# Stick-breaking attention on one core: value products ordered behind the scores of the unit five places later

## The chip, the cores and the metric

The kernel runs on one core of a Trainium2 chip. The metric is device time in microseconds (us) for one execution. A core has TensorE (PE, matrix products; PEld is its weight load), VectorE (DVE), ScalarE (ACT), GpSimd (POOL) and SyncE (SP, which here issues nearly all DMAs), each with its own in-order queue of instructions.

## The reference, cut to what matters

One layer on a sequence of 2048 positions and width 1024: RMS norm, one projection, four heads of differential attention and eight heads of stick-breaking attention, output projection with residual, and a SwiGLU feed-forward part. The part around the change is stick-breaking attention, per head and query `t`:

```python
z = jnp.einsum('bqhd,bkhd->bhqk', qb, k) * scale
mask = k_pos < q_pos                                   # strictly causal
log_1mb = jnp.where(mask, jax.nn.log_sigmoid(-z), 0.0)
rem = lax.cumsum(log_1mb, axis=3, reverse=True) - log_1mb
a = jnp.where(mask, jnp.exp(jax.nn.log_sigmoid(z) + rem), 0.0)
y = jnp.einsum('bhqk,bkhd->bqhd', a, v)
```

Each weight is thus sigmoid(z) times the product of sigmoid(-z) over the keys between it and the query.

## The kernel before, in words

The work is one stream without barriers, in two scopes. The first holds projections, attention and output projection, the second the feed-forward part, as products of 2x2 blocks. Products are made in float16 from operands that are split in a high and a low half, with three products for one.

Attention runs over eight groups `g` (`for g in range(NG)`, line 792). Groups 0 to 3 are the differential heads (`diff_attn`, line 460), groups 4 to 7 are pairs of stick-breaking heads (`sb_attn`, line 536). While a group is attended to, `advance` (line 708) emits the projection tiles of the next groups (`proj_tile`, line 313: 24 products of 384 columns at line 320 for each tile of 128 positions). In the last group the output projection (line 761) is emitted beside the attention.

A stick-breaking group is walked in 48 **units** (lines 577 to 587): for each of 16 query blocks `i` of 128 rows, for each 1024-column part `b` of the keys from the diagonal back, for each of the two heads `m`. A unit goes through these steps:

- `stage_a` (line 540), in chunks of up to 512 columns from the right: `score_chunk` (line 446) makes the scores in a PSUM tile `sc` (two products at line 448, and at the diagonal a third, line 450, that masks); ScalarE makes sigmoid(-z) into the SBUF tile `om` (line 554) and sigmoid(z) in place (line 555); VectorE scans the product from right to left (line 557) and multiplies (line 558). There are four `sc` tiles, and nine tiles `z4` for the `om` and `be` of all units.
- `split_t` (line 398): ScalarE casts the weights to float16 (line 89), GpSimd makes the low half (line 98), both in one of three buffers `s`; SP issues a DMA transpose into one of six buffers `aT` (line 403).
- `stage_b` (line 565), the unit's **values**: `pv` (line 453) multiplies `aT` by the values `v` into the PSUM tile `yp`, three products of 64 columns for each 128 keys (line 458, up to 24 for a unit); after the last unit of a row of query blocks `finish` (line 407) norms, transposes and stores to `ms`, which the output projection loads again.

The loop holds five units back in `pend` (`PD` = 5, line 39): it calls `stage_b` of a unit only after `stage_a` of the unit five places later. That is the order in which the program is written, not the order on the engines. The kernel is built with a scheduler that plays through an estimate of all durations and gives each engine, whenever it is free in that play, the ready instruction of highest priority. Priorities follow the written order, moved by the table `PRI` (line 32): `at` = 200 lifts all of `stage_a` ahead, and `pm` = -200 puts the projection products back; values (`pv` = 0) keep their place. So values can come out on TensorE ahead of scores of later units or behind them, and projections fill in.

What the scheduler makes is fixed at build time. On the chip every engine runs its list in order: an instruction whose input is late holds up all behind it on that engine.

Of the kernel before, what the change touches and what calls it, by code (L numbers as in the profile page):

```python
# [21 lines left out]
S, D, P = 2048, 1024, 128  # L22
# [37 lines left out]
def block(tc, a, out):  # L60
    nc = tc.nc
    PE, ACT, DVE, POOL, SP = nc.tensor, nc.scalar, nc.vector, nc.gpsimd, nc.sync
    top = ExitStack()
    with top:
# [186 lines left out]
        with ExitStack() as ph1:  # L251
# [189 lines left out]
            def fq(g, i):  # L441
                k = 2 if g == NG - 1 else 4
                return (i % k, k)

            @pri("sc")
            def score_chunk(G, sc, i, q, m, w, cut=False):
                for o in range(2):
                    PE.matmul(sc[:, : 128 * w].rearrange("p (t n) -> p t n", n=P), lhsT=G["q"][i // 4][:, 2 - 2 * o + m, i % 4, :], rhs=G["k"][q][:, m, 0:w, :], start=o == 0, stop=o == 1)  # L448
                if cut:
                    PE.matmul(sc[:, 128 * w - P : 128 * w], lhsT=idb[:], rhs=tri[:], start=False, stop=True, skip_group_check=True)  # L450

            @pri("pv")
            def pv(G, yp, y0, aT, b, n, o, wd, start, stop):
# [81 lines left out]

            def sb_attn(g, G):
                last = {}

                @pri("at")
                def stage_a(i, m, b):  # L540
                    L = (i + 1) * 128
                    n = min(1024, L - 1024 * b)
                    be, om = z4(), z4()
                    if b == i // 8:
                        DVE.memset(om[:, n : n + 1], 8192.0)
                    else:
                        DVE.tensor_copy(om[:, n : n + 1], last[m][:, 0:1])
                    last[m] = om
                    for c in range((n - 1) // 512, -1, -1):
                        lo, hi = 512 * c, min(512 * c + 512, n)  # L550
                        w = hi - lo
                        sc = ps.tile([P, 512], F32, tag="sc", bufs=4, name=nm("sc"))
                        score_chunk(G, sc, i, 2 * b + c, m, w // P, b == i // 8 and hi == n)
                        ACT.activation(om[:, lo:hi], sc[:, :w], AF.Sigmoid, scale=G["nkz"][:])  # L554
                        ACT.activation(sc[:, :w], sc[:, :w], AF.Sigmoid, scale=G["kz"][:])  # L555
                        ov = om[:, lo:hi][:, ::-1]
                        DVE.tensor_tensor_scan(ov, ov, sc[:, :w], om[:, hi : hi + 1], op0=ALU.mult, op1=ALU.bypass)  # L557
                        DVE.tensor_tensor(be[:, lo:hi], sc[:, :w], om[:, lo + 1 : hi + 1], ALU.mult)  # L558
# [669 lines left out]
```

## Time and profile before

| what | value |
|---|---|
| time, median of 3 runs (lowest, highest) | 2731.22 us (2727.44, 2734.09) |
| time of the profiled execution | 2740.3 us |
| its span, first to last instruction | 2738.5 us |
| mean granted TensorE clock | 0.967 |
| differential groups | until about 603 us |
| stick-breaking beside projections | about 603 to 1190 us |
| last group beside output projection | about 1190 to 1400 us |
| rest of output projection | to about 1458 us |
| feed-forward part | to the end |

An engine's busy time is the union of its instructions' times. A row of waits reads: engine, tile and line that waited, `<-` what ended the wait, then us in total, times, and the longest. A row of a timeline reads: start in us, duration in us, engine, line, operation, tiles written `<-` tiles read, shapes, count, and in brackets the engine's idle time before it and what ended it. Tile names come without numbers, so `z` stands for `om` and `be` of every unit, and `s` for the buffers of the cast. The end of an idle time is told by semaphores: where TensorE waits for a free `sc` tile, the row names the VectorE instruction that was last counted, which may be line 545, 547 or 558.

### The profile page before, as it was taken

To read this page: it belongs to the slowest core of one execution; us is meant where nothing else is said; L and a number is where in the kernel's file an instruction comes from. 1 tells how busy PE (TensorE), PEld (TensorE's weight loads), DVE (VectorE), ACT (ScalarE), POOL (GpSimd) and SP (SyncE) were. 2 spreads that over 40 slices of the span, in tenths; PEclk is the share of its full clock that TensorE was granted. 3 is DMA by queue.
4 is the path that set the end of the run, shared out by engine and by line. 5 is a ranking of instruction groups with operands and counts; after the bars stand their busy time and mean duration, and the time that the engine had idled before them with its cause. 6 is when DMAs were issued, how large, how long until landed. Compare 5 with 4: busy or idle time off the path is not lost.

```text
span 2738.5 us, 45414 instructions
## 1 busy us (share of the span) xinstructions
PE 2490.0 (91%) x17084; PEld 1409.8 (51%) x17084; DVE 1978.5 (72%) x3752; ACT 1353.3 (49%) x2539; POOL 1429.8 (52%) x1002
## 2 busy tenths in 40 slices
PE   7998989898978886889989898999999999999999
PEld 4655656565545553457775444444444444444444
DVE  6888879888888989987766777777786544434434
ACT  4665656566868778765644534344342212121121
POOL 2577677765554545546655566565664332222322
PEclk9999999998999997899999999999999999999999
DMA  6788787789998997997896665566657845635532
GB/s 227 199 164 178 151 198 164 180 171 200 208 201 184 212 186 151 203 192 208 213 289 256 220 234 191 208 221 216 231 204 283 316 158 181 220 128 193 192 116 93
DMA packets 646830, 543.52 MB, mean 198 GB/s; under 512 B 506369, under 2 KB 573953, under 8 KB 636369
## 3 DMA queue, kind: packets, MB, share of 16 engines
q1 hardware_dynamic: 644784, 538.53, 71.8%
q8 instruction: 134, 2.20, 0.3%
q0 software_dynamic: 512, 1.36, 0.2%
q10 hardware_dynamic: 1312, 0.72, 0.1%
q14 instruction: 88, 0.71, 0.1%
HBM read 261.08 MB, written 147.32 MB: 149 GB/s over the span
## 4 chain that ended last, share of the span: by engine, by line
PE 36%; DVE 9%; DMA 4%; POOL 3%; issue 3%; ACT 2%; SPq 0%; DVEq 0%; POOLq 0%; ACTq 0%
PE pd L1034 14%; PE pm L934 7%; PE pd L934 5%; PE pa L934 5%; DVE wd L215 2%; PE po L761 2%; DMA stages<-in_w_down_dram 1%; POOL stages L98 1%; DVE wu L215 1%; DMA aT<-s 1%; DVE z L557 1%; DVE cg L999 1%; DVE cg L98 1%; POOL s L98 1%; PE pj L320 1%
## 5 line engine op out<-in xcount | busy, mean ns | idle before, releaser
L98 POOL TENSOR_TENSOR s<-z,s 128x1024 f16<-128x1024 f32 (+7 forms) x288 | 474.4, 1655 | 320.1 <-ACT s L89 281.4
L320 PE MATMUL pj<-w,xt 128*128 128x384 f16 x3072 | 577.0, 336 | 19.2 <-DMA xt<-xs 5.6
L320 PEld LDWEIGHTS <-xt 128*128 128x128 f16 x3072 | 301.5, 101 | 233.1 <-issue 36.1
L557 DVE TENSOR_TENSOR_SCAN z<-z,sc 128x512 f32<-128x512 f32 (+3 forms) x320 | 356.1, 1114 | 72.1 <-ACT sc L555 68.8
L448 PE MATMUL sc<-kT,qT 128*128 128x512 f16 (+3 forms) x1280 | 348.3, 364 | 59.4 <-DVE z L558 23.7
L1034 PE MATMUL pd<-wd,act 128*128 128x512 f16 x1764 | 394.0, 381 | 7.2 <-DVE cu L968 7.1
L458 PE MATMUL yp<-v,aT 128*128 128x64 f16 (+1 forms) x4896 | 281.5, 209 | 82.3 <-DMA aT<-s 81.7
L458 PEld LDWEIGHTS <-aT 128*128 128x128 f16 x4896 | 245.4, 102 | 172.1 <-DMA aT<-s 110.4
L934 PEld LDWEIGHTS <-wg 128*128 128x128 f16 x1848 | 181.8, 98 | 228.1 <-issue 14.6
L934 PEld LDWEIGHTS <-wu 128*128 128x128 f16 x1848 | 180.8, 98 | 216.5 <-issue 2.0
L98 POOL TENSOR_TENSOR act<-cg,act 128x512 f16<-128x512 f32 x109 | 149.8, 1385 | 262.3 <-ACT act L993 262.3
L1034 PEld LDWEIGHTS <-act 128*128 128x128 f16 x1764 | 173.0, 98 | 216.6 <-issue 10.2
L89 ACT CAST s<-z 128x128 f16<-128x128 f32 (+7 forms) x216 | 170.3, 790 | 154.8 <-DMA aT<-s 72.9
L98 POOL TENSOR_TENSOR stages<-stages 128x512 f32<-128x512 f32 x97 | 172.9, 1783 | 120.1 <-DVE wg L215 41.4
L98 POOL TENSOR_TENSOR hs<-hs,cu 128x512 f32<-128x512 f32 x102 | 132.6, 1306 | 165.6 <-DVE hs L1040 62.7
L554 ACT ACTIVATE z<-sc,c 128x512 f32<-128x512 f32 (+3 forms) x320 | 204.4, 639 | 23.7 <-PE sc L448 18.9
L558 DVE TENSOR_TENSOR z<-sc,z 128x512 f32<-128x512 f32 (+3 forms) x320 | 193.7, 606 | 8.5
L555 ACT ACTIVATE sc<-sc,c 128x512 f32<-128x512 f32 (+3 forms) x320 | 196.5, 614 | 0.0
L1040 DVE SCALAR_TENSOR_TENSOR hs<-pd,c,hs 128x512 f32<-128x512 f32 x144 | 106.5, 748 | 118.5 <-PE pd L1034 113.6
L761 PE MATMUL po<-wo,mt 128*128 128x256 f16 x1536 | 180.7, 275 | 12.3 <-DVE xf L764 6.8
L993 ACT CAST act<-cg 128x512 f16<-128x512 f32 x126 | 76.9, 616 | 231.4 <-DVE cg L999 192.7
L934 PE MATMUL pm<-X,wu 128*128 128x512 f16 x792 | 179.1, 379 | 1.8 <-ACT cg L979 1.7
(241 smaller groups left out, 4109.1 us busy)
## 6 DMA issues: line engine op xcount, KB each, us to landing
xt<-xs SPq DMA_DIRECT2D x112, 512.0 KB, 4.4
hs<-hd SPq DMA_DIRECT2D x72, 512.0 KB, 4.5
hd<-hs SPq DMA_DIRECT2D x56, 512.0 KB, 5.8
split<-wg SPq DMA_DIRECT2D x11, 1792.0 KB, 6.9
split<-wu SPq DMA_DIRECT2D x11, 1792.0 KB, 6.7
split<-wd SPq DMA_DIRECT2D x11, 1792.0 KB, 6.8
wg<-split SPq DMA_DIRECT2D x11, 1792.0 KB, 7.4
wd<-split SPq DMA_DIRECT2D x11, 1792.0 KB, 9.1
```

The costliest lines, as they stand in the source:

```text
L89: ACT.copy(dst, src)
L98: (DVE if e == "D" else POOL).tensor_tensor(dst, a_, b_, op)
L320: PE.matmul(pj[:, :384], lhsT=xv[:, xi, kt, :], rhs=G["w"][:, wi, kt, :], start=n == 0, stop=n == 23)
L448: PE.matmul(sc[:, : 128 * w].rearrange("p (t n) -> p t n", n=P), lhsT=G["q"][i // 4][:, 2 - 2 * o + m, i % 4, :], rhs=G["k"][q][:, m, 0:w, ...
L458: PE.matmul(yp[:, y0 : y0 + wd], lhsT=aT[:, a_, :], rhs=v[:, v_ : v_ + wd], start=start and j == 0 and q == 0, stop=stop and j == nb - 1 a ...
L554: ACT.activation(om[:, lo:hi], sc[:, :w], AF.Sigmoid, scale=G["nkz"][:])
L555: ACT.activation(sc[:, :w], sc[:, :w], AF.Sigmoid, scale=G["kz"][:])
L557: DVE.tensor_tensor_scan(ov, ov, sc[:, :w], om[:, hi : hi + 1], op0=ALU.mult, op1=ALU.bypass)
L558: DVE.tensor_tensor(be[:, lo:hi], sc[:, :w], om[:, lo + 1 : hi + 1], ALU.mult)
L761: PE.matmul(po[:, sl], lhsT=mt[:, kt, P * xi : P * xi + P], rhs=wos[2 * h + n][wi][:, kt, :], start=q == 0, stop=q == 23)
L934: PE.matmul(ps_[:].rearrange("p (t n) -> p t n", n=P), lhsT=wv[:, wo, wi, 128 * kt : 128 * kt + 128], rhs=X[xo][:, :, xi, kt, :], start=st ...
L1034: PE.matmul(po[:], lhsT=act[:, ao, xi, 128 * j : 128 * j + 128], rhs=W["d"][:, wo, wi, :], start=start and u == 0 and q == 0, stop=u == nu ...
```

## The change

`score_chunk` hands back its last product; `stage_a` collects these in a list `front` for the group; `stage_b` becomes a wrapper that issues the old body, now `stage_c`, inside `tc.issue_after(front[-1])`. That adds an ordering edge, without a semaphore, from the last score product collected so far to each instruction of `stage_c` on the same engine, TensorE. These are the value products and the transposes of `finish`. As `stage_b` is called after `stage_a` of the unit five places later, that is the unit whose scores they now follow; the five units left at the end of a group follow the last scores of the group.

```diff
             def score_chunk(G, sc, i, q, m, w, cut=False):
                 for o in range(2):
-                    PE.matmul(sc[:, : 128 * w]..., start=o == 0, stop=o == 1)
+                    last = PE.matmul(sc[:, : 128 * w]..., start=o == 0, stop=o == 1)
                 if cut:
-                    PE.matmul(sc[:, 128 * w - P : 128 * w], lhsT=idb[:], rhs=tri[:], ...)
+                    last = PE.matmul(sc[:, 128 * w - P : 128 * w], lhsT=idb[:], rhs=tri[:], ...)
+                return last.ins
...
             def sb_attn(g, G):
                 last = {}
+                front = []
...
-                        score_chunk(G, sc, i, 2 * b + c, m, w // P, b == i // 8 and hi == n)
+                        front.append(score_chunk(G, sc, i, 2 * b + c, m, w // P, b == i // 8 and hi == n))
...
                 def stage_b(i, m, b, n, aT):
+                    with tc.issue_after(front[-1]):
+                        stage_c(i, m, b, n, aT)
+
+                def stage_c(i, m, b, n, aT):
                     r, k = fq(g, i)
```

`score_chunk` is also called by `diff_attn`, which does not use what it hands back. The scheduler gets the edges before it plays, so the order of all engines in the stick-breaking part is made anew.

More of the change, by code (lines that the diff above doesn't have):

```diff
@@ L447, in score_chunk @@
                 for o in range(2):
-                    PE.matmul(sc[:, : 128 * w].rearrange("p (t n) -> p t n", n=P), lhsT=G["q"][i // 4][:, 2 - 2 * o + m, i % 4, :], rhs=G["k"][q][:, m, 0:w, :], start=o == 0, stop=o == 1)
+                    last = PE.matmul(sc[:, : 128 * w].rearrange("p (t n) -> p t n", n=P), lhsT=G["q"][i // 4][:, 2 - 2 * o + m, i % 4, :], rhs=G["k"][q][:, m, 0:w, :], start=o == 0, stop=o == 1)
                 if cut:
-                    PE.matmul(sc[:, 128 * w - P : 128 * w], lhsT=idb[:], rhs=tri[:], start=False, stop=True, skip_group_check=True)
+                    last = PE.matmul(sc[:, 128 * w - P : 128 * w], lhsT=idb[:], rhs=tri[:], start=False, stop=True, skip_group_check=True)
+                return last.ins
             @pri("pv")
```

## The prediction

> **What bounds the kernel now.** I read the page first, for the two halves of the span, and then the time before 1400 us by windows, because the diff touches only the stick-breaking groups.
>
> ```profile
> span 2738.5 us, 45414 instructions
> PE 2490.0 (91%) x17084; PEld 1409.8 (51%) x17084; DVE 1978.5 (72%) x3752; ACT 1353.3 (49%) x2539; POOL 1429.8 (52%) x1002
> ...
> 603.00:1190.00 587.00, 479.96 (x4801) 298.49 (x4800) 522.95 (x942) 457.90 (x883) 306.54 (x196) 0.90 0.96 192
> 1190.00:1400.00 210.00, 187.05 (x2016) 154.34 (x2014) 155.28 (x244) 129.04 (x225) 126.94 (x87) 0.98 0.86 213
> ```
>
> The columns of the last two rows are busy time of PE, PEld, DVE, ACT and POOL, then granted clock, DMA share and GB/s. From 603 to 1190 us (stick-breaking beside the projections of later groups) VectorE is busy for 522.95 of 587 us, 89%: it is the bound, and the change can only win its idle 64 us. From 1190 to 1400 us (the last group beside the output projection) TensorE is busy for 187.05 of 210 us, also 89%, and VectorE for only 155.28: there TensorE's order is the bound. So I price the two stages apart, and take from each the list of waits, first for 603 to 1190:
>
> ```profile
> PE yp L458 <- DMA aT<-s: 47.8, 44, 2.9
> ACT s L89 <- DMA aT<-s: 45.3, 36, 3.9
> DVE z L557 <- ACT sc L555: 39.7, 47, 4.6
> ...
> PE sc L448 <- DVE z L558: 22.3, 24, 2.4
> PE sc L448 <- DVE z L545: 15.2, 22, 2.0
> ...
> ACT z L554 <- PE sc L448: 10.2, 9, 2.7
> PE sc L448 <- DVE z L547: 8.7, 8, 1.8
> ...
> ACT z L554 <- PE sc L450: 2.8, 3, 1.4
> ```
>
> A row gives total us, times, and the longest. TensorE stands 47.8 us before value products (line 458) whose transposed weights aT have not landed; those are the waits the new edge is aimed at. But it also stands 22.3 + 15.2 + 8.7 = 46.2 us before scores (line 448) that wait for VectorE to free one of the four PSUM tiles. That is what an engine off the bound looks like: ahead of VectorE nearly as often as it is late. Of VectorE's idle time 39.7 us are before a scan (line 557) that waits for ScalarE's second sigmoid. ScalarE itself waited for scores only 10.2 + 2.8 = 13.0 us, and 45.3 us for the buffer s that a transpose had not yet read. Only the 13.0 us can come from the order on TensorE at first hand.
>
> How a value wait gets to VectorE is best seen once, in the timeline around 720 us (PE, then ACT and DVE), with two windows of 3.4 us below it:
>
> ```profile
> 719.56 0.70 PE L458 MATMUL yp<-v,aT 128*128 128x64 f16 x18 [2.08 <-DMA aT<-s]
> ...
> 721.58 4.09 PE L320 MATMUL pj<-w,xt 128*128 128x384 f16 x18
> 725.51 0.19 PE L458 MATMUL yp<-v,aT 128*128 128x64 f16 x1
> 725.54 0.59 PE L448 MATMUL sc<-kT,qT 128*128 128x512 f16 x2
> ...
> 726.17 0.69 ACT L554 ACTIVATE z<-sc,c 128x512 f32<-128x512 f32 x1 [0.58 <-PE sc L448]
> 726.76 0.66 ACT L555 ACTIVATE sc<-sc,c 128x512 f32<-128x512 f32 x1
> ...
> 727.45 1.65 DVE L557 TENSOR_TENSOR_SCAN z<-z,sc 128x512 f32<-128x512 f32 x2 [2.06 <-ACT sc L555]
> ...
> 716.80:720.20 3.40, 1.32 (x24) 0.77 (x23) 3.37 (x6) 2.36 (x6) 0.00 (x0) 1.00 1.17 197
> 720.20:723.60 3.40, 3.40 (x21) 1.89 (x18) 3.40 (x6) 2.48 (x6) 1.17 (x2) 0.50 1.10 197
> ```
>
> TensorE waits 2.08 us for aT and is busy for only 1.32 of 3.40 us. In the next 3.40 us its clock is granted at 0.50; the 18 projection products take 4.09 us, the score behind them starts late at 725.54, and VectorE idles 2.06 us. So a wait costs something at the bound only when it is followed by half clock and by a long stretch of projection ahead of the next score.
>
> **The change, part by part.** It adds and removes no instruction on any engine. Each value group of a unit (up to 24 products at line 458) gets an edge, without a semaphore, behind the last score product issued when the loop reaches it, which is the score of the unit five later. In the built programs I counted, for each of the 192 value groups, how many later units have all their scores ahead of it on TensorE: before, 105 have fewer than five (63 four, 30 three, 12 fewer) and the mean is 4.47; after, 8 have (the ends of groups), and the mean is 5.23. So the change does what it says, and that it does not is no rival. It moves about half of the value groups by one to three units. From there the scheduler places all else anew on all five engines in the stick-breaking part; the order of TensorE before it and of the feed-forward products after it is the same.
>
> *First term, waits removed in 603 to 1190.* I laid the 44 waits of the row above over the built order: about 16.5 us of them, a share of 0.35, stand before values with fewer than five places, and the rest before values with five or more, which the edge does not move. The one at 719.56 is of these. If the scores' lateness goes in that share, ScalarE gets 0.35 x 13.0 = 4.5 us back, and VectorE with it: **-4.5 us**, between 0 (all hidden by VectorE) and -13.0.
>
> *Second term, 1190 to 1400.* The waits there:
>
> ```profile
> PE yp L458 <- DMA aT<-s: 8.4, 8, 2.6
> PE po L761 <- DVE xf L764: 6.8, 9, 1.8
> ...
> 1203.34 0.54 PE L458 MATMUL yp<-v,aT 128*128 128x64 f16 x6 [0.92 <-DMA aT<-s]
> ...
> 1395.07 0.87 PE L458 MATMUL yp<-v,aT 128*128 128x64 f16 x24 [1.24 <-DMA aT<-s]
> ```
>
> Here the mean number of places goes from 3.31 to 4.83 over the last group, the largest move, and output projection (line 761) is there to fill TensorE. The first and the last of the 8 waits stay: the 0.92 us stands before a value with five places already, the 1.24 us before the last unit's, which no score follows. **-6 us** for the other six, between 0 and -8.4. It reaches the end because after the last value the chain of waits goes straight through TensorE:
>
> ```profile
> 1388.43 6.59 DMA aT<-s
> ...
> 1442.92 14.93 PE po L761 x120
> ```
>
> Values that come later push nothing out here: by the built orders 459 output-projection products stand behind the last value before and 504 after, and only the last 192 of them need the last values. What is late next is the 6.8 us on VectorE's additions, which stays.
>
> *Third term, longer stretches between scores.* Values that may not fill the time before a score leave it to projections and come in one piece afterwards. Between two neighbouring scores of the first 160 units there are 10 stretches with 22 or more projection products before, and 22 after. Whether one hurts follows from these rows:
>
> ```profile
> L557 DVE TENSOR_TENSOR_SCAN z<-z,sc 128x512 f32<-128x512 f32 x224 | 285.3, 1274 | 37.1 <-ACT sc L555 35.3
> L558 DVE TENSOR_TENSOR z<-sc,z 128x512 f32<-128x512 f32 x224 | 153.6, 686 | 5.2
> ...
> 854.65 1.95 PE L320 MATMUL pj<-w,xt 128*128 128x384 f16 x11
> ```
>
> Four score tiles give VectorE 4 x (1.27 + 0.69) = 7.8 us of work. A score tile needs 0.59 us on TensorE and 0.69 + 0.66 us of sigmoids before VectorE may read it, so TensorE can be away for about 5.9 us. At full clock 22 products take 22 x 1.95 / 11 = 3.9 us, and that is hidden. At half clock they take 22 x 4.09 / 18 = 5.0 us and the values with them over 1 us more: then VectorE idles. The clock of 0.90 in this stage, with steps of 0.50 and 1.00, means half clock for about 20% of it. The worst price of one is the 2.06 us above, so 12 further stretches cost at most 25 us, and 20% of that is **+5 us**, which I take. Below, a gain of 8.5 us is possible (13.0 - 4.5, if scores that nothing blocks come early throughout).
>
> *Buffers.* Later values free their aT (six of them) later, and a transpose could wait for one. From 620 to 1390 us:
>
> ```profile
> SPq L403 <- POOL s L98: 195.8, 102, 6.8
> ...
> SPq L403 <- PE yp L458: 1.9, 1, 1.9
> ...
> 979.80 0.83 PE L458 MATMUL yp<-v,aT 128*128 128x64 f16 x23
> ...
> 982.69 1.24 SPq L403 DMA_TRANSPOSE aT<-s  x1
> ```
>
> Transposes wait for their data, and once for a value. The last two rows are a value and the transpose of the unit six later, the closest such pair (2.1 us apart); over all 168 pairs of the four groups the transpose was issued 14 us after the later of the value and of the score five places on, at the median. So **0 us**, with a bound on the other side in the rivals. The edge itself is no instruction, and costs nothing.
>
> Sum: -4.5 - 6 + 5 = -5.5 us. The profiled execution took 2740.3 us (2738.5 in the span), so 2734.8 for its like. It stands 9.1 above the median of the three timed runs, 2731.22, and 2731.22 - 5.5 = 2725.7; I forecast **2725**.
>
> A rule that would change this is in the Trainium skill, page "TensorE: Matmul & The Clock Gate", section "HAM oscillation — how this bites in real kernels": TensorE keeps its full clock as long as it has no idle gap beyond about 3.4 us. By that rule alone no wait of these lists (the longest 2.9 us) would halve the clock, and the third term would be nothing, the sum -10.5 us. The trace differs: the 2.08 us wait above was followed by 0.50. The measurement decides, and this is a rival below with a small chance.
>
> **The rivals.**
>
> *Nothing at the bound.* VectorE's 523 us stay, transposes land when they did, and TensorE turns one kind of waiting (47.8 us) into the other (46.2 us). For it: 89% busy VectorE, and that two thirds of the value waits stand at five places or more. Against it: the second stage, where TensorE is the bound. Time: 2731.
>
> *Half clock in the long stretches* (the other side). Values and projections now stand behind scores that wait for a PSUM tile, so that TensorE idles in one piece, falls to 0.50 and then runs its longer stretch at half speed, at the place where the example at 720 us shows it. Price: 25 us less the 10.5 us of the first two terms, 2746. It decides from the point where most of the 22 stretches meet half clock, or the granted clock of 603 to 1190 falls from 0.90 to below 0.85. Against it: fewer waits for aT also means fewer falls of the clock.
>
> *Transposes wait for aT.* If slack of 2 us is what counts and not 13, transposes back up, ScalarE's 45.3 us before its cast grows by a quarter, and VectorE's idle time with it: +11, 2742.
>
> *All scores in time.* The first term at its bound of 13.0 us and the second at 6: 2712.
>
> *Short waits leave the clock alone.* If TensorE's clock falls for another reason than waits of some 2 us, the longer stretches cost nothing and the first two terms stand alone: 2731.2 - 10.5 = 2721. Against it: 0.50 right behind the 2.08 us.
>
> **How the numbers follow.** Within 0.2% (5.5 us) is about what a measurement of this kernel can tell from no change, so the forecast lies just outside it. Chances: the forecast 0.33 (of it 0.06 within 0.2%), all scores in time 0.10, short waits 0.03, nothing at the bound 0.27, half clock 0.20, transposes 0.07. That makes faster 0.40, same 0.33, slower 0.27. The two ends, 2712 and 2746, belong to the range, which I widen by 3 us below, as the spread of the runs shown: 2709 to 2746. The forecast's own range is 2718 to 2731.
>
> **What would show it.** First term: ScalarE's waits for scores in stick-breaking fall from 13.0 us to about 8, and VectorE's 39.7 us before the scan to about 35. Second: the value waits of the last group fall from 8.4 us to about 2, and the last output projection ends some 6 us earlier against the start of that group. Third: the granted clock in the stage stays at 0.88 to 0.91, and score waits of TensorE on VectorE rise above 46 us, since TensorE gets there sooner. Slower with a clock below 0.85 is the half-clock rival; slower with more waits of line 403 on line 458 is the buffers. It is all wrong if VectorE's busy time changes, or if the difference lies in the diff-attention or the feed-forward part, whose order on TensorE is unchanged.

## The result and the profile after

The change made the kernel slower by 0.3%: 2742.03 us median (20 runs, 2734.84 to 2745.91) against 2731.46 for the kernel before (20 runs, 2727.44 to 2739.26); the ratio is 1.0030, 95% interval [1.0022, 1.0038]. Two further batches of runs put it at 1.0013 [1.0003, 1.0022] and 1.0025 [1.0011, 1.0039].

The two profiled executions hide this. The one of before took 2740.3 us, more than any of the 20 runs above; the one after took 2738.5, the seventh shortest of its own 20. So whole spans are not compared here but stages, and for each kernel over several traces: before twice, the change three times. The marks are the first score of group 4, the ends of the scans of units 120 and 160, with the multiplication behind each scan (units counted through the four groups, 0 to 191), the end of the last value products (unit 191), and the points at which 168 and 500 gate or up products of the feed-forward part have been issued.

| stage, us | before | change | difference of means |
|---|---|---|---|
| first score of group 4 to scan of unit 120 | 437.3, 433.4 | 437.0, 436.4, 436.0 | +1.1 |
| to scan of unit 160 | 152.4, 151.8 | 153.7, 150.6, 150.7 | -0.5 |
| to the end of the last values | 202.6, 202.3 | 196.3, 197.4, 197.6 | -5.4 |
| to the 168th gate or up product | 108.1, 108.4 | 120.6, 120.6, 120.1 | **+12.2** |
| to the 500th | 127.9, 127.9 | 123.4, 123.3, 124.2 | -4.3 |
| to the end | 1106.6, 1104.2 | 1103.0, 1103.8, 1104.6 | -1.6 |

The differences add up to +1.5 us, less than the 3.6 to 8.2 us of the three ratios; the first trace of before, as said, is of a long execution. The stick-breaking stages are as long as before or, in the last group, shorter. What is lost is lost behind the last value, in the **handover**: the rest of the output projection and the first feed-forward products. A third of it comes back soon after. And the gain in the last group is in good part a shift: 45 products of the output projection, about 5 us of work, move from there into the handover. The last group, the handover and the stretch to the 500th product together are 2.5 us longer than before.

The stage from 603 to 1190 us in the change, by windows (busy us of PE, PEld, DVE, ACT, POOL, then granted clock, DMA share, GB/s), with the last group below it:

```profile
603.00:1190.00 587.00, 468.90 (x4732) 294.58 (x4730) 520.27 (x937) 456.60 (x880) 303.40 (x195) 0.92 0.92 191
1190.00:1400.00 210.00, 187.97 (x2088) 156.42 (x2087) 152.99 (x248) 130.19 (x227) 132.39 (x90) 0.99 0.88 217
```

VectorE's busy time is what it was (522.95 before), and the clock did not fall (0.90 before). The list of waits of the change in 603 to 1190:

```profile
PE sc L448 <- DVE z L560: 47.8, 46, 2.9
DVE z L559 <- ACT sc L557: 40.7, 50, 3.3
...
PE yp L459 <- DMA aT<-s: 22.7, 19, 2.4
...
PE sc L448 <- DVE z L547: 19.5, 23, 2.3
...
PE sc L448 <- DVE z L549: 9.2, 9, 1.8
...
ACT z L556 <- PE sc L450: 5.1, 5, 1.5
...
ACT z L556 <- PE sc L448: 3.3, 6, 1.2
```

Lines 459, 556, 557 and 559 are 458, 554, 555 and 557 of before; 547, 549 and 560 are 545, 547 and 558. The edge did what it is for, and more than forecast: TensorE's waits for aT before values went from 47.8 to 22.7 us, ScalarE's for scores from 13.0 to 8.4. But TensorE now waits 76.5 us (47.8 + 19.5 + 9.2) for a free PSUM tile, where it was 46.2, and VectorE's wait before the scan stayed: 39.7 before, 40.7 now. One kind of TensorE's waiting was turned into the other. In the last group, from 1190 to 1400 us, its waits at values are nearly what they were (8.4 before):

```profile
PE yp L459 <- DMA aT<-s: 7.9, 7, 2.2
```

In the handover the two kernels look like this. First before, TensorE's timeline from the output projection on:

```profile
1442.92 14.93 PE L761 MATMUL po<-wo,mt 128*128 128x256 f16 x120 [1.99 <-DVE wo L764]
...
1523.89 1.94 PE L1108 MATMUL xtr<-id,bx 128*128 128x128 f32 x8 [9.36 <-DVE bx L223]
```

Then the change (L767 is the output projection, L940 the gate and up products; L1108 above is the transposes of the norm before the feed-forward part):

```profile
1423.93 5.40 PE L767 MATMUL po<-wo,mt 128*128 128x256 f16 x48
1432.63 8.17 PE L767 MATMUL po<-wo,mt 128*128 128x256 f16 x48 [3.29 <-DVE c L171]
1441.27 5.40 PE L767 MATMUL po<-wo,mt 128*128 128x256 f16 x48 [0.47 <-DVE wo L770]
...
1458.24 4.48 PE L940 MATMUL pm<-X,wg 128*128 128x512 f16 x20
1462.56 0.59 PE L940 MATMUL pa<-X,wg 128*128 128x512 f16 x2
1462.99 2.78 PE L767 MATMUL po<-wo,mt 128*128 128x256 f16 x24
...
1478.59 4.45 PE L940 MATMUL pd<-X,wg 128*128 128x512 f16 x12 [2.02 <-DMA X<-xcd]
```

In the second listing three things are new. TensorE waits 3.29 us for VectorE and then needs 8.17 us for 48 products that took 5.40 just before. The last 24 output-projection products stand behind 22 gate products (4.48 + 0.59 us). And TensorE waits 2.02 us for an X that a DMA brings. The wait of 9.36 us at 1523.89, on the other hand, is gone. VectorE's timeline shows where the 3.29 us come from:

```profile
1423.97 0.47 DVE L770 SCALAR_TENSOR_TENSOR wo<-po,c,wo 128x256 f32<-128x256 f32 x1
...
1424.54 1.92 DVE L212 TENSOR_SCALAR wg<-stages,c 128x1024 f16<-128x1024 f32 x1
...
1429.77 1.75 DVE L215 SCALAR_TENSOR_TENSOR wg<-sx,c,wg 128x512 f16<-128x512 f32 x1
...
1432.10 0.47 DVE L770 SCALAR_TENSOR_TENSOR wo<-po,c,wo 128x256 f32<-128x256 f32 x1
```

Between two additions that free PSUM tiles of the output projection, the scheduler has put most of the split of a gate weight, 1424.5 to 1431.5. The products of the first tile ended at 1429.3 (1423.93 + 5.40); their addition had to queue. So an edge on TensorE, in stick-breaking attention, changed VectorE's order in another part.

SP's timeline tells the third difference, here before:

```profile
1458.40 0.32 SPq L766 DMA_DIRECT2D hd<-xf  x1
1458.81 0.38 SPq L1120 DMA_DIRECT2D X<-xcd  x1
...
1461.86 0.90 SPq L1099 DMA_DIRECT2D bx<-hd  x2
```

and here in the change:

```profile
1466.32 0.32 SPq L772 DMA_DIRECT2D hd<-xf  x1
1469.11 0.32 SPq L922 DMA_DIRECT2D split<-wd  x1
1469.52 0.38 SPq L1126 DMA_DIRECT2D X<-xcd  x1
...
1470.92 2.59 SPq L1105 DMA_DIRECT2D bx<-hd  x2
```

The last store of the output projection, the seventh X load and the loads for the transposes leave 8 to 11 us later in these two traces, although the last values ended 6 us earlier, and the X load now stands behind a store (`split`) that waits for VectorE.

### The profile page after: what moved, and what is told of

Read it like the earlier page. It is cut to its first block, busy times and chain, and to the rows that moved or that the text cites. A ratio compares the mean times of both kernels' runs of the same rounds, so it can differ in the third digit from the quotient of the medians.

```text
span 2736.7 us, 45401 instructions
## 1 busy us (share of the span) xinstructions
PE 2480.4 (91%) x17084; PEld 1407.3 (51%) x17084; DVE 1973.9 (72%) x3752; ACT 1353.5 (49%) x2539; POOL 1430.2 (52%) x1002
## 4 chain that ended last, share of the span: by engine, by line
PE 33%; DVE 8%; DMA 5%; POOL 3%; issue 2%; ACT 2%; SPq 0%; DVEq 0%; POOLq 0%; ACTq 0%
PE pd L1040 14%; PE pm L940 7%; PE pd L940 5%; PE pa L940 5%; DVE wd L215 2%; PE po L767 1%; DMA stages<-in_w_down_dram 1%; POOL stages L98 1%; DMA X<-xcd 1%; DMA aT<-s 1%; DVE wu L215 1%; DMA hd<-hs 1%; DVE z L559 1%; DVE cg L1005 1%; DVE cg L98 1%
## 5 line engine op out<-in xcount | busy, mean ns | idle before, releaser
L320 PE MATMUL pj<-w,xt 128*128 128x384 f16 x3072 | 567.8, 333 | 20.8 <-DVE st L330 7.0
L940 PEld LDWEIGHTS <-wg 128*128 128x128 f16 x1848 | 181.5, 98 | 229.0 <-issue 14.5
L940 PEld LDWEIGHTS <-wu 128*128 128x128 f16 x1848 | 181.0, 98 | 221.8 <-issue 8.2
L98 POOL TENSOR_TENSOR act<-cg,act 128x512 f16<-128x512 f32 x109 | 150.6, 1392 | 263.6 <-ACT act L999 263.6
L767 PE MATMUL po<-wo,mt 128*128 128x256 f16 x1536 | 181.3, 277 | 11.5 <-DVE xf L770 6.9
L448 PEld LDWEIGHTS <-qT 128*128 128x128 f16 x1280 | 105.7, 99 | 163.8 <-DVE z L560 65.5
```

The source lines that it names most:

```text
L98: (DVE if e == "D" else POOL).tensor_tensor(dst, a_, b_, op)
L320: PE.matmul(pj[:, :384], lhsT=xv[:, xi, kt, :], rhs=G["w"][:, wi, kt, :], start=n == 0, stop=n == 23)
L448: last = PE.matmul(sc[:, : 128 * w].rearrange("p (t n) -> p t n", n=P), lhsT=G["q"][i // 4][:, 2 - 2 * o + m, i % 4, :], rhs=G["k"][q][:, ...
L767: PE.matmul(po[:, sl], lhsT=mt[:, kt, P * xi : P * xi + P], rhs=wos[2 * h + n][wi][:, kt, :], start=q == 0, stop=q == 23)
L940: PE.matmul(ps_[:].rearrange("p (t n) -> p t n", n=P), lhsT=wv[:, wo, wi, 128 * kt : 128 * kt + 128], rhs=X[xo][:, :, xi, kt, :], start=st ...
```

## The experiments

The first theory was the **handover**: the loss is the 22 gate products ahead of the last 24 of the output projection. Its rival was that the **order redrawn** in the stick-breaking part costs it (the forecast's third term). In the expectations the first is also called 'tail', the second 'values'; later and narrower theories have letters. All ratios are to before on the same chip; the experiments ran on five chips.

### Where in the kernel: before again, and the edge in parts

`e1_before_again` is before unchanged, for a second trace.

> The kernel before, unchanged, for a second trace: its profiled execution of 2740.3 us lay 9 us above the median, and it has an idle time of 9.4 us of TensorE before the transposes of line 1108 (at 1514 to 1524 us) that need not be there each time. If that idle time is what set it apart, this one takes 2728 to 2734 us, has less than 3 us there, and stands at the same times as the first trace up to 1500 us within 2 us. If the execution was slow throughout, the times differ already before 1400 us.

It took 2732.2 us, and its stages are the second numbers in the table above. The idle time was there again (9.29 us), so it does not set the first trace apart; the two differ before 1400 us already (437.3 against 433.4 us up to unit 120).

`e2_edge_early` and `e3_edge_last` have the edge in groups 4 to 6 only, and in group 7 only:

```diff
-                    with tc.issue_after(front[-1]):
+                    with tc.issue_after(front[-1]) if g < NG - 1 else nullcontext():
```

(`g == NG - 1` in the second).

> The edge in groups 4 to 6 only, not in the last group. Theory tail (the loss is where the output projection goes over into the feed-forward part, whose order the scheduler made anew): little or nothing is lost here, 0 to +4 us against before, the more as 12 gate products still stand ahead of the last output projection products (22 after the change, none before). Theory values (later values cost time in the stick-breaking groups themselves, by half clock or by buffers): +6 to +10 us, as three of the four groups have the edge.

> The edge in the last group only; everything on TensorE up to that group is as before. Theory tail: the whole loss is here, +7 to +11 us, with the last scores some 5 us earlier than before and the feed-forward part some 5 us later. Theory values: a quarter of the loss or less, 0 to +3 us.

`e2_edge_early` gave 1.0032 [1.0018, 1.0046], `e3_edge_last` 1.0027 [1.0018, 1.0037]: each half loses as much as the whole, so they do not add up. They lose in different places. With the edge in the last group, the 12 us are in the handover again (119.7 us from the last values to the 168th product). With the edge in the early groups the handover takes 109.9, but the stretch from the scan of unit 144 to that of unit 160 takes 73.8 us instead of 65.3 and 64.8. There, first before (its second trace, TensorE):

```profile
1174.56 6.15 PE L320 MATMUL pj<-w,xt 128*128 128x384 f16 x24 [1.47 <-DVE st L330]
...
1181.24 0.71 PE L448 MATMUL sc<-kT,qT 128*128 128x128 f16 x4
...
1181.96 3.74 PE L320 MATMUL pj<-w,xt 128*128 128x384 f16 x22
```

and `e2_edge_early`:

```profile
1187.99 6.32 PE L320 MATMUL pj<-w,xt 128*128 128x384 f16 x24 [2.67 <-DVE st L330]
...
1195.01 3.58 PE L320 MATMUL pj<-w,xt 128*128 128x384 f16 x21
...
1198.65 0.71 PE L448 MATMUL sc<-kT,qT 128*128 128x128 f16 x4
```

Both have 24 projection products at half clock behind a wait (0.26 us each instead of 0.17). Before has four score products between these and the next 22; in the other order they come only after 45. That this is what costs the 9 us is read from the rows; no run moved the four score products back.

### Is it the handover: the same edges with one more

`e4_after_tail` is the change with an edge that puts the first gate products behind the last output-projection product:

```diff
-                                    PE.matmul(po[:, sl], ...)
+                                    spare[-1] = PE.matmul(po[:, sl], ...)
...
-                sg = gate(W, X, in_gate)
+                with tc.issue_after(spare[-1].ins) if i == 0 else nullcontext():
+                    sg = gate(W, X, in_gate)
```

> The change, and beside it a second edge: the first gate product of the feed-forward part is issued behind the last product of the output projection, as it was before. Theory tail: the loss goes, and what the values won in the last group (6 us) shows, 2722 to 2732 us, that is -8 to +1 us against before; the last output projection ends before 1458 us and the load of the seventh X tile is issued 8 us sooner than after the change. Theory values: still +7 to +10 us.

1.0001 [0.999, 1.0011]: the loss is gone. The long wait of the change is not:

```profile
1433.31 6.81 PE L767 MATMUL po<-wo,mt 128*128 128x256 f16 x48 [3.29 <-DVE c L171]
1441.76 5.40 PE L767 MATMUL po<-wo,mt 128*128 128x256 f16 x48 [1.64 <-DVE wo L770]
```

So the wait for VectorE and the half clock behind it, the first of the three new things, are not the loss that this edge takes away. But the edge, too, moves more than the 22 products: the seventh X load stands ahead of the `split` store again, and the orders of all engines differ from the change's, from 1458 us on TensorE until about 1580 us. Run again as `e10_after_tail_again` in another batch:

> The change with the first gate products behind the last output-projection product, once more. Theory A (the change's loss is the order in its tail, which this order mends): ratio 0.9995 to 1.001, and again about 111 us from the end of the last values to the 168th gate product. Rival C (the first run's 1.0001 was luck, the edge costs in the stick-breaking part): ratio 1.0015 to 1.003.

1.0009 [0.9998, 1.0021], with 110.8 us in the handover (first run 111.4, the change 120). By its ratio alone this run could not be told from the lowest of the change's three (1.0013 [1.0003, 1.0022]); the stage can. The same edge beside the edge in the last group only, `e11_last_tail`:

> The edge in the last group only, as in edge-last (+0.27%), with the first gate products behind the last output-projection product. Theory A: the loss goes, ratio 0.999 to 1.001. Rival C: it stays, ratio 1.002 to 1.0035.

0.9996 [0.9985, 1.0007], against 1.0027 without it on another chip; handover 112.3 us instead of 119.7. And beside the edge in the early groups, `e5_early_tail`:

> Edge in the first three stick-breaking groups only, as in the run edge-early (+0.32%), and the first gate products of the feed-forward part kept behind the last output-projection product (12 stood ahead of it in edge-early). The instruction order of every engine is that of edge-early up to the output projection's end. Theory 'handover' (the whole loss comes from gate products ahead of the last output projection): ratio to before 0.999 to 1.001. Rival 'order redrawn' (projection tiles ahead of scores at the start of the last group, run at half clock): ratio 1.0025 to 1.0035; from the scan end of unit 144 to that of unit 160 again about 73 us instead of 65, and from the end of the last values to the 168th gate product 108 to 110 us as before.

1.0036 [1.0025, 1.0048], with 74.2 us from unit 144 to 160. The rival was right here: this kernel's loss is the order at the start of the last group; its handover took 107.9 us, as before's. So there are two different losses. For the change itself, whose stretch from 144 to 160 is as short as before's (64 to 65 us), it is the handover.

### Are gate products ahead enough: the reverse

`e6_before_late` is before with 24 gate products put by hand ahead of the last 24 of the output projection; SP's order is not touched. `early` makes the first two products of `gate`, 12 instructions each, which `gate` then leaves out:

```diff
+                            if (t, h, n) == (NT - 1, 1, 1):
+                                early()
...
-                                    PE.matmul(po[:, sl], ...)
+                                    with tc.issue_after(ahead2[-1]) if ahead2 else nullcontext():
+                                        PE.matmul(po[:, sl], ...)
```

> The kernel before, with 24 gate products put ahead of the last 24 output-projection products; the order of every engine up to there is that of before, and SP's order is unchanged throughout. Theory 'handover': the last store of the output projection, the seventh X load and the loads behind it go out 5 us later or more, TensorE waits for X and before the transposes of line 1108, and the time is 4 to 8 us above before (ratio 1.0015 to 1.003); from the end of the last values to the 168th gate product 112 to 117 us instead of 108. Rival 'the 24 products in another order cost nothing, the loss needs the late output projection': ratio 0.999 to 1.001.

0.9994 [0.9983, 1.0005], and the handover took 105.4 us, 3 less than before. The simple theory fell. TensorE's row from the last values to the last output-projection product, before (second trace):

```profile
1389.90:1452.10 62.20, 56.14 (x495) 49.25 (x493) 34.12 (x56) 19.19 (x24) 30.90 (x20) 0.97 0.93 349
```

and in `e6_before_late`:

```profile
1393.40:1457.10 63.70, 59.65 (x519) 50.80 (x518) 34.20 (x56) 19.31 (x24) 31.02 (x20) 1.00 0.91 344
```

24 more products, and only 1.5 us longer: they went into time in which TensorE waited (6.1 us idle before, 4.1 here; the wait of 1.99 us ahead of the 120 products is gone) and ran at a better clock. The same row for the change:

```profile
1389.73:1465.77 76.04, 69.29 (x563) 57.62 (x562) 38.44 (x69) 26.62 (x31) 35.01 (x24) 0.93 0.80 293
```

It is 13.8 us longer than before's. About 5 us of that are the 45 products from the last group (5.40 us for 48) and about 5 the 22 gate products (4.48 + 0.59). TensorE is idle there for 6.75 us, but most of it earlier; behind the 48-product blocks just ahead of the gate products it waits 0.35 to 0.47 us, so they find no gap. In the change's traces the last output-projection product comes 75.5 to 76.0 us after the last values, and 71.8 and 71.2 with the gate products held back: they delay it by 4.3 us.

`e9_before_hold` takes the other suspect alone: 45 more output-projection products behind the last values (504, as in the change), by an edge in before.

```diff
-                        PE.matmul(yp[:, y0 : y0 + wd], ...)
+                        lastv[0] = PE.matmul(yp[:, y0 : y0 + wd], ...)
...
-                                    PE.matmul(po[:, sl], ...)
+                                    with tc.issue_after(lastv[0].ins) if t == 11 or (t, h, n) == (10, 1, 1) else nullcontext():
+                                        PE.matmul(po[:, sl], ...)
```

> The kernel before, with 45 more output-projection products kept behind the last value product, 504 as in the change (before: 459); the stick-breaking order up to 1200 us is that of before, and VectorE's additions in the tail stay single, as in before. Theory A (work is only moved): from the scan end of unit 120 to the end of the last values 4 to 6 us shorter than before's 354, from there to the 168th gate product as much longer than before's 108; ratio 0.999 to 1.001. Rival B (a late output projection by itself delays the feed-forward part's loads): ratio 1.0015 to 1.004.

1.0005 [0.9994, 1.0017]: the total as Theory A has it, the parts not. The last group took 201.5 us, hardly less than 202.4 (the mean over five traces with before's order), and the handover 108.4, no more than before. TensorE's row of the last group up to the last values, before (second trace):

```profile
1187.58:1389.92 202.34, 180.39 (x1921) 147.53 (x1918) 150.43 (x238) 126.33 (x216) 122.82 (x85) 0.98 0.86 213
```

and `e9_before_hold`:

```profile
1192.82:1394.36 201.54, 176.02 (x1876) 143.87 (x1872) 148.70 (x236) 124.40 (x213) 122.24 (x84) 0.98 0.84 210
```

45 products and 4.4 us of work fewer, and TensorE waits 3.6 us more instead (25.5 us against 22.0). Its waits at values in these windows are, before:

```profile
PE yp L458 <- DMA aT<-s: 7.7, 9, 2.3
```

and in `e9_before_hold`:

```profile
PE yp L460 <- DMA aT<-s: 11.8, 10, 3.6
```

In the change the same work leaves the last group without more of them (7.9 us), and the group is 5 us shorter. That is what the edge wins there.

### Is it SP's order: the X load

With gate products and late work each ruled out by itself, the X load behind the `split` store was the next suspect; `e4_after_tail` had moved it, too. `e13_x_first` is the change with that store put behind the X load, `e14_before_x_late` before with the X load behind that store, by a later call and an edge in `load_x`. The first diff leaves out that `load_x` now notes the seventh X load in `rows` and that an older edge counts one place further; the second, the edge itself. In the second the load of the down weights is also called ahead of `tick(1)`, a step of the norm, and so the edit moves more than the X load:

```diff
-                    SP.dma_start(split[fg, "gud".index(nme)], ...)
+                    with tc.issue_after(rows[0].ins) if (fg, nme) == (0, "d") else nullcontext():
+                        SP.dma_start(split[fg, "gud".index(nme)], ...)
```

```diff
-            load_x(0, XL[6:])
...
-            tick(1)
             load_now(0, 0, "d", W)
+            load_x(0, XL[6:])
+            tick(1)
```

> The change with one edge on SP: the seventh X load goes out ahead of the store of the split down weights, as in before (in the change it stands behind that store, which waits for VectorE: the load went out 3.2 us after the last store of the output projection instead of 0.4, and landed 9.0 us after its issue instead of 5.7). TensorE's order is that of the change until well after the last output-projection product, with 22 gate products ahead of the last 24. Theory D (the loss is this queue order): TensorE's wait of 2.0 us for X goes, from the end of the last values to the 168th gate product 111 to 115 us instead of 120.6, ratio to before 0.9995 to 1.001. Rival E (the loss is what comes earlier in the tail, 3.3 us before the output projection and half clock behind it): 118 to 121 us, ratio 1.0015 to 1.003.

> The reverse: the kernel before, with the seventh X load behind the store of the split down weights on SP; the order of every engine up to the end of the output projection is that of before. Theory D: the load goes out 3 us later or more, TensorE waits for X, from the end of the last values to the 168th gate product 112 to 118 us instead of 108; ratio 1.0005 to 1.003. Rival E: 107 to 110 us, ratio 0.9995 to 1.0005.

Theory D fell on both; rival E had the total of `e13_x_first` and the handover of `e14_before_x_late` right, not the rest. `e13_x_first` stayed at 1.0029 [1.0019, 1.0038]: the 2.0 us wait went and the handover took 116.7 us instead of 120, but the next stretch took 129.1 instead of 123.6. And `e14_before_x_late` was *faster* than before: 0.9971 [0.996, 0.9982], the handover unchanged at 108.5 and the next stretch 120.2 instead of 127.9. TensorE in that run:

```profile
1467.66 3.99 PE L1110 MATMUL xtr<-id,bx 128*128 128x128 f32 x16 [4.99 <-DVE xrs L150]
...
1505.37 1.91 PE L1110 MATMUL xtr<-id,bx 128*128 128x128 f32 x16
```

and SP:

```profile
1447.46 0.32 SPq L766 DMA_DIRECT2D hd<-xf  x1
...
1462.62 0.32 SPq L916 DMA_DIRECT2D split<-wd  x1
1462.98 0.43 SPq L1123 DMA_DIRECT2D X<-xcd  x1
1480.10 0.40 SPq L1101 DMA_DIRECT2D bx<-hd  x1
1483.82 0.49 SPq L1101 DMA_DIRECT2D bx<-hd  x1
```

The second pair of `bx` loads leaves 33 and 36 us after the `hd` store; in before it is 40 and 45 us (1498.40 and 1503.86, with a `split` store at 1499.64 between them). The second transposes start without a wait, where before waits 9.36 us. The change has a little of this, its pair leaves 38 and 40 us after the store, and the wait is gone there too. That is where its 4.3 us come back: over all 20 traces, the stretch from the 168th to the 500th product took 120.2 to 124.2 us in the eight in which TensorE waits for at most 1.3 us before the second transposes, and 126.2 to 129.4 us in the twelve in which it waits for 3.0 to 10.5. What in `e14_before_x_late` took the wait away, the place of the X load or the order that the scheduler redrew with it (on TensorE until about 1580 us), no run tells apart.

`e13_x_first` also shows why the gate products ahead seem to be lost time in the change. From the last output-projection product to the 168th gate or up product, `e13_x_first`:

```profile
1468.10:1508.20 40.10, 36.90 (x178) 18.12 (x177) 26.18 (x34) 19.72 (x26) 24.70 (x16) 0.96 0.60 210
```

and `e4_after_tail`:

```profile
1462.20:1501.80 39.60, 39.60 (x202) 19.73 (x200) 30.44 (x36) 22.02 (x28) 27.14 (x17) 1.00 0.57 202
```

24 products fewer and as long: what TensorE did ahead of the last store saves nothing behind it. It is idle for 3.2 us there, before the first transposes, whose data come by the loads that follow that store, and its clock is 0.96 instead of 1.00.

`e15_change_third` gave the size of the change's loss beside these two:

> The change beside the two others on one chip, for the size of its loss, which stands at 1.003 and 1.0013. Theory D and rival E alike: 1.0012 to 1.0032, 120 us from the end of the last values to the 168th gate product.

1.0025 [1.0011, 1.0039]. `e8_change_again` is the run of the batch before:

> The change once more, beside the others on one chip and for a second trace. Both theories: ratio 1.002 to 1.004. Theory 'handover': from the end of the last values to the 168th gate product about 120 us again, from the first score of group 4 to the scan end of unit 120 about 437. Rival 'order redrawn': the first figure varies and the loss appears in the stick-breaking stages.

1.0013 [1.0003, 1.0022], below the 1.002 expected. Both have 120 us in the handover, as the theory had it.

### Do the values' waits matter at all

`e7_tail_three` is `e4_after_tail` with the values three places behind instead of five (`PD` = 3): 103 value groups have fewer than five places again, as 105 had before.

> The change with the values three places behind instead of five (103 of 192 value groups have fewer than five places again, mean 4.57), and the first gate products behind the last output-projection product. Theory 'nothing at the bound': TensorE's waits for aT at values in the stage from 603 us rise to 40 us or more, and the stage from the first score of group 4 to the scan end of unit 120 stays at 437 us, plus or minus 3; the time within 0.15% of before. Rival 'value waits count': that stage is 5 us longer or more, the time 0.2 to 0.5% above before.

0.9994 [0.9984, 1.0004]. From 603 to 1190 us, its list of waits:

```profile
DVE z L559 <- ACT sc L557: 39.7, 44, 4.4
PE yp L459 <- DMA aT<-s: 36.5, 35, 3.3
```

The waits at values came out at 36.5 us, not the 40 expected, and VectorE's wait before the scan at 39.7. Over before (two traces), the change and this run the value waits are 47.8, 46.7, 22.7 and 36.5 us, and VectorE's waits 39.7, 42.9, 40.7 and 39.7: no connection. The stage up to unit 120 took 437.3 us, as expected.

### What the edge is worth by itself, and a version that beats both

`e12_three_and_late` joins the edge at three places with the gate products of `e6_before_late`; `e16_three_late_again` is the same once more:

> A try for a version that beats both: the edge at three places instead of five, and 24 gate products ahead of the last 24 output-projection products (both runs were at 0.9994). If the two add up: 0.998 to 0.9995. If both were nothing: 0.9995 to 1.0005.

> The version that stood at 0.9989 [0.9978, 1.0]: the edge at three places, and 24 gate products ahead of the last 24 output-projection products. If it beats before: 0.998 to 0.9995 again, its interval below 1. If the first result was luck: 0.9995 to 1.0005.

0.9989 [0.9978, 1.0] and 0.9985 [0.9974, 0.9995]: faster than before by a little over 0.1% (the first interval touches 1). The two do not simply add up: the largest part lies in the stretch to the 500th product (121.8 and 123.4 us against 127.9), where no more than 1.3 us of the wait before the second transposes is left.

Last, the change and before were given the handover that had turned out best, `e17_change_tail_x_late` (both extra edges) and `e18_before_x_late_again` (the X load alone), on one chip:

> The change with both edges at the handover: first gate products behind the last output-projection product, and the seventh X load behind the store of the split down weights (that edge alone took 0.29% off the kernel before). Theory F (the edge of the change itself wins some 5 us between the scan end of unit 160 and the end of the last values, and all its loss is the handover): 0.995 to 0.998, as fast as before-x-late or up to 5 us faster; from the scan end of unit 160 to the 168th gate product 308 to 310 us, 120 us more to the 500th. Rival G (what the last group wins is only moved, as 3 us into the tail, and the first groups lose 1 to 2 us): 0.998 to 1.000, 3 to 8 us slower than before-x-late.

> The kernel before with the seventh X load behind that store, beside the run above on one chip. If the first result holds: 0.996 to 0.998.

0.9991 [0.9979, 1.0002] and 0.9978 [0.9966, 0.999], 2730.85 against 2726.92 us. Rival G was nearer: the edge wins nothing by itself, and may lose a little (the intervals overlap). Its last group is 4.3 us shorter (197.8 against 202.1), its handover 3.7 longer (114.3 against 110.6), and the 500th product comes 122.8 us later, not 120.2. The best version is before with the X load late: 0.9971 and 0.9978, without the edge of the change.

## Why the prediction was wrong

The forecast of 2725 us, faster, was wrong in sign. 2742 lies in the range; it is the very number of the rival "Transposes wait for aT" and near the 2746 of the half-clock rival, but that is luck. Neither gives the reason: ScalarE's wait before its cast, which the first has grow by a quarter from 45.3 us, fell to 37.5, and the clock, which the second has fall below 0.85, rose to 0.92.

- **First term, -4.5 us: nothing seen.** The stages up to unit 160 are +1.1 and -0.5 us. Its first link held, and by more: the value waits fell by 25.1 us, not 16.5, and ScalarE's waits for scores to 8.4 us ("about 8"). The failed step is "ScalarE gets 0.35 x 13.0 = 4.5 us back, and VectorE with it". VectorE's wait before the scan stayed, 39.7 before and 40.7 now: TensorE waits for free PSUM tiles instead, 76.5 us against 46.2. The rival "nothing at the bound" describes this stage, and `e7_tail_three` shows it once more.
- **Second term, -6 us: the size came, not the way.** The last group became shorter by 5.4 us, but its waits at values are 7.9 us where 2 were forecast. Work left it, 45 output-projection products, and `e9_before_hold` shows that the same work leaving without the edge gains 1 us only. The step that failed is "It reaches the end because after the last value the chain of waits goes straight through TensorE": the chain was read from the order before, and in the new one the 45 products and the 22 gate products stand behind the last value, 76.0 us to the last output-projection product instead of 62.
- **Third term, +5 us: not in the change.** The clock rose to 0.92, and the stage up to unit 160 is no longer than before by more than the spread of traces. The mechanism seems to exist, by the rows, at one place in `e2_edge_early` and `e5_early_tail`, with 45 products in a row; the stretch is some 9 us longer there, four times the 2.06 us taken as the worst.
- **Buffers, 0 us: right.** Transposes waited once for a value, for 2.1 us (1.9 before).
- **What the sum lacked: the handover, +12.2 us and then -4.3.** The text says "the order of TensorE before it and of the feed-forward products after it is the same". It is not: 22 gate products moved ahead of the output projection's end, and the orders differ until about 1580 us, more than 100 us into the feed-forward part, on VectorE and SP too. The scheduler that "places all else anew on all five engines" was allowed for in the stick-breaking part alone. Of the signs of being all wrong, the one that "the difference lies in the diff-attention or the feed-forward part" was met in part: the loss lies in the end of the output projection and the start of the feed-forward part.

Shown is where the loss is (three traces against two), and that it goes with an edge that holds back the gate products and redraws the order behind it (two pairs, with two runs of the first). Shown too is that no single piece does it alone in the kernel before: gate products ahead and late output projection cost nothing there, and the version with the late X load is faster. That it takes their meeting, no gap on TensorE to take up the gate products and loads that hang on the last store, is how the rows read, but it is not shown: no run built it up in before. Left open is a small rest: the stages of the traces add up to less than the times say. Traces with the edge in the early groups take 436.0 to 438.8 us up to unit 120 (nine, mean 437.6), those without 432.8 to 439.6 (eight, mean 435.7). That may be the 4 us by which `e17_change_tail_x_late` is behind `e18_before_x_late_again`, but these spreads don't settle it.

The prediction weighed a rule of the Trainium skill, page "TensorE: Matmul & The Clock Gate", section "HAM oscillation — how this bites in real kernels": the clock stays full as long as no idle gap exceeds some 3.4 us. The traces differ from it once more: half clock stood behind a wait of 2.67 us in `e2_edge_early` (rows above) and one of 3.29 us in the change (rows below).

## What to carry to other kernels

An ordering edge in a scheduled kernel is no instruction, but it lets the scheduler redraw everything behind it: compare the built orders of all engines to the end of the program, and look first at the handover to the next part, where stores, loads and small VectorE steps hang on each other. A wait that goes is a gain only if the engine at the bound waits less; here 25 us of TensorE's waits went and 30 us of another wait of TensorE's came. And price work that moves out of a stretch where it arrives: 45 products that cost nothing in one order of the tail (`e9_before_hold`) sat in a tail 12 us longer in another.

## What the runs showed of the hardware

The clock behind a short wait, in the change, by windows of 3.4 us around the wait of 3.29 us:

```profile
1425.80:1429.20 3.40, 3.40 (x33) 3.03 (x31) 3.40 (x6) 0.50 (x1) 0.64 (x2) 1.00 1.01 402
1429.20:1432.60 3.40, 0.14 (x2) 0.00 (x0) 3.40 (x7) 0.00 (x0) 2.77 (x2) 0.84 1.02 292
1432.60:1436.00 3.40, 3.37 (x17) 2.31 (x17) 2.23 (x6) 1.05 (x2) 3.40 (x4) 0.50 1.02 386
1436.00:1439.40 3.40, 3.40 (x22) 2.57 (x21) 3.40 (x4) 0.82 (x1) 1.71 (x1) 0.66 1.01 418
```

The granted clock is 1.00 ahead of the wait, 0.50 in the 3.4 us behind it and 0.66 in the next; 48 products took 8.17 us instead of 5.40. In `e8_change_again` it was 3.53 us and then 8.02. Little of these 2.8 us was lost: in `e4_after_tail` the same wait was followed by 6.81 us, but then TensorE waited 1.64 us for VectorE, and from the end of the wait to the next block it was 8.45 us there and 8.64 in the change.

It is not the length of one wait that decides. In the traces the granted clock is 0.50 or 1.00 and changes only at points that lie a multiple of 3.41 us apart. Cut into these steps, before and the change (first traces) have 1378 steps at full clock in which TensorE was busy for 60% or more, and none was followed by half clock; of 56 in which it was busy for less than 40%, 48 were. The seventh X load landed 9.0 us after its issue in the change, behind the `split` store, and 5.7 us in before (second trace). And the executions differ before the part that was changed: the first score of group 4 came at 599.3 to 605.7 us in the 17 traces of kernels with values five places behind, though TensorE's order up to there is the same in all of them, a spread as large as the effect looked for.
